# Low parts of the mixer's first 32 weight tiles: made in the first feed-forward block and kept in HBM, or made in the mixer

## The chip, the cores and the metric

The kernel runs on one core of one Trainium2 chip. The metric is the device time of one execution in microseconds (us), as the median of several runs. The engines are TensorE (PE, with its weight load PEld), VectorE (DVE), ScalarE (ACT), GpSimd (POOL) and SyncE (SP), which issues most of the DMAs.

## What is computed

One encoder layer in float32 on 512 tokens of width 1024: a half-step feed-forward block, a mixer of two head groups, a second half-step feed-forward block, and a last norm.

```python
x = x + 0.5 * swiglu(rms_norm(x, ffn1_norm[l]), ffn1_w_gate[l], ffn1_w_up[l], ffn1_w_down[l])
h = rms_norm(x, mix_norm[l])
proj = h @ w_in[l]
qkv_a, z_a, a_a, b_a, qkv_b = jnp.split(proj, split_at, axis=-1)
o_a = gdn_mixer(qkv_a, z_a, a_a, b_a, conv_w[l], a_log[l], dt_bias[l], gdn_norm_w[l])
o_b = dilated_mixer(qkv_b, q_norm_w[l], k_norm_w[l], rel_bias)
x = x + jnp.concatenate([o_a, o_b], axis=-1) @ w_out[l]
...
```

swiglu is (silu(x @ w_gate) * (x @ w_up)) @ w_down with 2816 hidden columns. gdn_mixer is a gated delta rule with four heads of 128, in both directions, with a short convolution, normalized queries and keys, and a triangular solve in each chunk of tokens. dilated_mixer is softmax attention of eight heads of 64 over bands, at three dilations.

## The kernel before

All activations are held transposed, in tiles of 128 features by 512 tokens. Every large product is made of three matmuls (mm3): each factor is split into a high part, rounded to fp32r by a copy on ACT, and a low part, the difference, made by a subtraction on DVE; the three are high by high, high by low and low by high.

In the feed-forward blocks wload (L167) brings a weight tile of 128 x 1024 (raw, two buffers) by a DMA on SP, casts it on ACT (L178) and subtracts on DVE (L179). The first block's gate and up phase, 44 such tiles, lasts until about 250 us, its down phase until 369.6; the mixer lasts until about 734, the second block's gate and up phase until 975.

In the mixer the weights come as 76 tiles of 128 x 512, in the order of the list plan (L185 to L189): two tiles for each projection of ORDER, K0 Q0 K1 Q1 K3 Q2 K2 Z0 Q3 V0 Pa0 V1 Z3 V2 V3 v0 and so on, then 16 for the output projection and 4 for the second block. Tiles 14 and 15 are Z0's, 16 and 17 Q3's, 24 and 25 Z3's, 28 and 29 V3's, 42 and 43 Pa1's. wnext (L211) keeps up to three tiles wsp in use; each is made by split (L228): a cast on ACT (L229), then a subtraction on DVE (L226). The raw data (wrw, two halves of one tile) is loaded ahead by fetch (L198) on SP; a half is free again when its subtraction is done. mm3 uses the high part in its first two matmuls and the low part in the third.

PE's order in the mixer is fixed by hand: interleave runs streams of work by due times, and PEQueue ties each PE instruction to the one before. The other engines' orders are set by a scheduler that weighs when an instruction could run; each engine, and SP's queue, then works strictly in that order. For each head h of the delta rule, decay makes gb on ACT (L561), multiplies it on PE (pdc) and takes the exponential into M; the stage behind the convolution squares keys and queries on ACT (L611), forms pkk and pkq on PE, scales M on DVE (L638), and stores blocks of M into the HBM tensor D1, eight DMAs on SP for each head (L644). When all four heads are there, solve (L824 to L854) loads MM from D1, runs a triangular solve on DVE, stores ZM and ZN and loads M and ZT from them. vtok (L700) are transposed values of the delta rule, made on ACT; the attention's scores go through an exponential into L on ACT (L164).

Of the kernel before, what the change touches and what calls it, by code (L numbers as in the profile page):

```python
# [10 lines left out]
F32 = mybir.dt.float32  # L11
F32R = mybir.dt.float32r
AF = mybir.ActivationFunctionType
ALU = mybir.AluOpType
AX = mybir.AxisListType

P = 128
T = 512
# [15 lines left out]
N_MASK = 768  # L34
LV0, LVG, SCG, ATG = 9.0, 0.625, 0.8, 0.55
GIN, VGO, VGV, PRG, NRG, VTG, VBG, OPG, OTG, FNG, SVG, SSD, SST, VTP, LVH = 9.5, 16.5, 4.0, 0.5, 6.0, 3.5, 3.5, 13.5, 0.75, 10.5, 0.75, 8.0, 0.6, 3.0, 1.3
PRI = 0, 1, 2, 4, 3, 5
ORDER = "rs@1 pa@3 K0 ab gt@2 Q0 K1 bi Q1 pc@3 g0 K3 Q2 K2 g1 Z0 g2 Q3 g3 V0 Pa0 V1 Z3 V2 V3 v0 Pb0 Z2 Z1 Pb1 v1 Pa1 v3 Pa2 Pb2 v2 Pb3 Pa3 oa"

# [50 lines left out]
def encoder_layer(ctx, tc, xT, gu1, dn1, win, wab, wo1, wo2, gu2, dn2, cols, relb, masks, onehot, lnc, sel, out):  # L90
    nc = tc.nc
    te, ve, se, gp, sy = PEQueue(tc, nc.tensor), nc.vector, nc.scalar, nc.gpsimd, nc.sync
# [4 lines left out]
    WF = {"pool": None}  # L97
    tp = ctx.enter_context(tc.tile_pool(name="tp", bufs=2))
    ps = ctx.enter_context(tc.tile_pool(name="ps", bufs=2, space=bass.MemoryType.PSUM))
    dr = ctx.enter_context(tc.tile_pool(name="dr", bufs=1, space=bass.MemoryType.DRAM))  # L100
# [18 lines left out]
    def palt(name):  # L119
        nalt[0] += 1  # L120
        return (pmm, pfl, prg)[nalt[0] % 3](name)

    def tmp(tag, name, n=T, dt=F32, bufs=2):
        return tp.tile([P, n], dt, tag=tag, name=name, bufs=bufs)
# [42 lines left out]
    def wload(src, n, k, low=False, parts=1, then=None):  # L167
        w = n * k
        raw = WF["pool"].tile([P, 1024], F32, tag="raw", name="wraw", bufs=2)
        if low:  # L170
            hi, lo = (wtile(nm) for nm in ("whi", "wlo"))
        else:
            hi, lo = (WF["pool"].tile([P, 1024], F32R, tag=nm, name=nm, bufs=2) for nm in ("whi", "wlo"))
        sv = src.rearrange("p a b -> p (a b)")
        for i in range(parts):
            s = slice(i * w // parts, (i + 1) * w // parts)
            act["lastf"] = sy.dma_start(out=raw[:, s], in_=sv[:, s])
            se.copy(hi[:, s], raw[:, s])  # L178
            ve.tensor_tensor(out=lo[:, s], in0=raw[:, s], in1=hi.bitcast(F32)[:, s], op=ALU.subtract)  # L179
            if then is not None:  # L180
                then(i)
        return (hi[:, :w].rearrange("p (a b) -> p a b", b=k),
                lo[:, :w].rearrange("p (a b) -> p a b", b=k))

    first = {"K": 4, "Q": 0, "V": 8, "Z": 12, "Pa": 16, "Pb": 20, "v": 24}  # L185
    plan = [win[first[u[:-1]] + int(u[-1]), :, 4 * i:4 * i + 4] for u in ORDER.split() if u[:-1] in first
            for i in range(2)]
    plan += [wo1[d, :, 4 * u:4 * u + 4] for d in range(4) for u in range(3)] + [wo2[d] for d in range(4)]
    plan += [gu2[0, j, :, 4 * u:4 * u + 4] for j in range(2) for u in range(2)]  # L189
    nw, got, fetched, ready, wraw = [0], [0, 0], [], [], []  # L190

    def wtile(name, dt=F32R):

        nw[0] += 1
        t, n = ("wb", 1) if nw[0] % 4 == 0 else ("wa", 3)
        return wp.tile([P, 1024], dt, tag=t, name=name, bufs=n)

    def fetch(i):  # L198
        if i < len(plan):
            r = wraw[0][:, i % 2 * T:(i % 2 + 1) * T]  # L200
            sy.dma_start(out=r, in_=plan[i].rearrange("p a b -> p (a b)"))
            fetched.append(r)
# [8 lines left out]
    def wnext():  # L211

        while got[0] < len(plan) and len(ready) < 3:
            t = wp.tile([P, 1024], F32R, tag="wa", name="wsp", bufs=3)
            ready.append(t)
            got[0] += 1
        while got[1] < got[0] - (got[0] < len(plan)):
            i = got[1] - got[0] + len(ready)
            split(ready[i][:, 0:T], ready[i][:, T:2 * T], fetched.pop(0))
            got[1] += 1  # L220
            fetch(got[1] + 1)
        t = ready.pop(0)
        return [t[:, i * T:(i + 1) * T].rearrange("p (a b) -> p a b", b=P) for i in range(2)]

    def sub(o, a, b):
        ve.tensor_tensor(out=o, in0=a, in1=b.bitcast(F32), op=ALU.subtract)  # L226

    def split(hi, lo, src):  # L228
        se.copy(hi, src)  # L229
        sub(lo, src, hi)  # L230

    def mm3(o, wh, wl, rh, rl, start, stop):
        te.matmul(o, lhsT=wh, rhs=rh, start=start, stop=False)
        te.matmul(o, lhsT=wh, rhs=rl, start=False, stop=False)
        act["mm"] = te.matmul(o, lhsT=wl, rhs=rh, start=False, stop=stop)
# [11 lines left out]
    class Norm:  # L247
# [28 lines left out]
        def rstd(self):  # L276
# [4 lines left out]
            preload()  # L281
            rsq(R, pr, 1024.0)

    def ffn(gu, dn, norm, nxt, then=None, late=False, mid=None):
        with tc.tile_pool(name="wf", bufs=2, reuse_waits="tile") as wf, \
                tc.tile_pool(name="hp", bufs=1, reuse_waits="tile") as hp:
            WF["pool"] = wf
            hh = [hp.tile([P, T], F32R, name=f"hh{f}") for f in range(NF)]
            hl = [hp.tile([P, T], F32R, name=f"hl{f}") for f in range(NF)]
            wait = []  # L290
            for f in range(NF):
                pg, pu = palt("pg"), palt("pu")
                for j, pt in ((0, pg), (1, pu)):
                    if f == 0 and late:
                        for u in (0, 4):
                            wh, wl = wnext()
                            for k in range(u, u + 4):
                                mm3(pt, wh[:, k - u], wl[:, k - u], xh[k], xl[k], k == 0, k == NKT - 1)
                        continue
                    first = then if f == 0 and j == 0 else None  # L300
                    wh, wl = wload(gu[f, j], NKT, P, True, 4 if first else 2 if f == 0 else 1, first)
                    for k in range(NKT):
                        mm3(pt, wh[:, k], wl[:, k], xh[k], xl[k], k == 0, k == NKT - 1)
                wait.append((f, pg, pu))
                if f == (0 if late else 1):
                    with tc.issue_after(norm.last.ins):
                        for k in range(NKT):
                            norm.sq(k)
                    norm.rstd()
                if f == 0 and not late:  # L310
                    continue
                for e, pg, pu in wait:
                    g, u = tmp("g", "g"), tmp("u", "u")
                    ve.tensor_tensor(out=g, in0=pg, in1=R, op=ALU.mult)  # L314
                    silu(g, g)
                    ve.tensor_tensor(out=u, in0=pu, in1=R, op=ALU.mult)  # L316
                    ve.tensor_tensor(out=u, in0=u, in1=g, op=ALU.mult)
                    split(hh[e], hl[e], u)
                wait = []
            for d in range(NKT - 1 if late else NKT):  # L320
                pd = palt("pd")
                for f0, n in ((0, 8), (8, 8), (16, 6)):
                    wh, wl = wload(dn[d, :, f0:f0 + n], n, P)
                    for i in range(n):
                        f = f0 + i
                        mm3(pd, wh[:, i], wl[:, i], hh[f], hl[f], f == 0, f == NF - 1)
                ve.scalar_tensor_tensor(out=x[d], in0=pd, scalar=0.5, in1=x[d], op0=ALU.mult, op1=ALU.add)
                nxt(d)
            if late:
                d = NKT - 1  # L330
                ws = [wload(dn[d, :, f0:f0 + n], n, P, f0 == 0) for f0, n in ((0, 8), (8, 8), (16, 6))]
                for i in range(2):
                    pd, s = palt("pd"), slice(256 * i, 256 * i + 256)
                    for f in range(NF):
                        wh, wl = ws[f // 8]
                        mm3(pd[:, 0:256], wh[:, f % 8], wl[:, f % 8], hh[f][:, s], hl[f][:, s], f == 0, f == NF - 1)
                        if (i, f) in ((0, 15), (1, 4)):
                            with tc.issue_after(act["mm"].ins):
                                mid(i)
                    ve.scalar_tensor_tensor(out=x[d][:, s], in0=pd[:, 0:256], scalar=0.5, in1=x[d][:, s], op0=ALU.mult,  # L340
                                            op1=ALU.add)
                nxt(d)
# [15 lines left out]
    def after1(d):  # L358
        n2.add(d)
        sy.dma_start(out=x_d[d], in_=x[d])  # L360

    ffn(gu1, dn1, n1, after1, bring)
    with tc.issue_after(act["lastf"].ins):
        sy.dma_start(out=mk, in_=masks)

    wopen()
    with ExitStack() as mctx:
# [827 lines left out]
        ss = [fins(), chain(), after(), norms(), att(), px()]  # L1195
        interleave([ss[i] for i in PRI])
        te.fixed = False
# [132 lines left out]
```

## Time and profile before

| what | value |
|---|---|
| median of 3 runs | 1108.98 us (1108.09 to 1111.36) |
| the profiled execution | 1109.54 us, its span 1107.8 us |
| mean granted clock of PE | 0.991 |
| PE busy in the span | 1071.4 us, 97% |
| DVE busy | 614.7 us, 55% |
| ACT busy | 443.6 us, 40% |
| HBM read and written | 102.39 and 8.96 MB, 101 GB/s |

The span is what the trace shows of the execution; 1.74 us of its time lie outside. The profile page cuts the span into 40 slices of 27.7 us: PE is at nine tenths or more in all but eight or so, most of which lie in the mixer, where DVE is the next busiest. A timeline row gives an instruction's start, its length, the engine, the line, the operation with its output and inputs, a count where neighbours are put together, and in brackets how long its engine had been idle and what ended that. Clocks are shares of the full 2.4 GHz.

### The profile page before, as it was taken

What the parts mean: (1) busy time and instruction counts of PE and PEld (TensorE: products, weight loads), DVE (VectorE), ACT (ScalarE), POOL (GpSimd) and SP (SyncE); (2) the same over time, 40 slices, a digit from 0 to 9 for tenths busy, and PEclk for the clock granted to TensorE, in tenths of its full rate; (3) what the DMA queues carried; (4) which work ended last, traced back from release to release, by engine and by line L of the source; (5) the groups of instructions that cost most, each with busy time, mean ns of one, the idle gap of its engine ahead of it and who ended that gap; (6) DMA issues with size and microseconds to landing.
All of it is one profiled execution on the core that took longest, in us unless ns stands there. A gap on an engine that the chain in (4) does not pass through costs nothing.

```text
span 1107.8 us, 14127 instructions
## 1 busy us (share of the span) xinstructions
PE 1071.4 (97%) x5394; PEld 881.4 (80%) x5394; DVE 614.7 (55%) x1113; ACT 443.6 (40%) x812; POOL 86.6 (8%) x123
## 2 busy tenths in 40 slices
PE   9999999999999989898999978999999999999996
PEld 7888888888888768776788866878888888888886
DVE  4544444443443497898677888685444444532223
ACT  6432222233222256434675766464232222332221
POOL 3000000000111212610000010000000000001001
PEclk9999999999999999999899999999999999999999
DMA  5222222234433133345422242233222223233332
GB/s 191 97 96 95 95 95 98 97 112 143 121 107 119 35 111 91 105 128 157 72 83 84 70 155 74 69 113 95 95 96 95 97 94 104 94 97 95 96 105 77
DMA packets 53235, 112.27 MB, mean 101 GB/s; under 512 B 17984, under 2 KB 20576, under 8 KB 53168
## 3 DMA queue, kind: packets, MB, share of 16 engines
q1 hardware_dynamic: 48976, 99.50, 29.1%
q0 software_dynamic: 2896, 10.25, 3.1%
q10 hardware_dynamic: 1296, 1.63, 0.5%
q8 instruction: 42, 0.69, 0.3%
q14 instruction: 25, 0.20, 0.1%
HBM read 102.39 MB, written 8.96 MB: 101 GB/s over the span
## 4 chain that ended last, share of the span: by engine, by line
PE 82%; DVE 9%; ACT 3%; issue 3%; DMA 2%; POOL 1%; DVEq 0%; SPq 0%; ACTq 0%; POOLq 0%
PE pg L52 22%; PE pd L52 22%; PE pu L52 22%; PE pc L50 3%; PE pd L50 2%; PE pqk L50 2%; PE ps L50 2%; PE pl L50 1%; DVE wsp L226 1%; PE pout L52 1%; DMA wrw<-in_win 1%; PE pT L50 1%; PE pvb L50 1%; PE pov L50 1%; PE pS L50 1%
## 5 line engine op out<-in xcount | busy, mean ns | idle before, releaser
L178 ACT CAST whi<-wraw 128x1024 fp32r<-128x1024 f32 (+1 forms) x138 | 137.6, 1000 | 424.7 <-issue 174.1
L179 DVE TENSOR_TENSOR wlo<-wraw,whi 128x1024 fp32r<-128x1024 f32 (+1 forms) x138 | 161.1, 1168 | 134.3 <-ACT whi L178 130.1
L52 PE MATMUL pd<-hh,whi 128*128 128x512 f32 (+1 forms) x374 | 141.2, 378 | 0.0
L52 PE MATMUL pd<-hh,wlo 128*128 128x512 f32 (+1 forms) x374 | 140.9, 377 | 0.0
L52 PE MATMUL pd<-hl,whi 128*128 128x512 f32 (+1 forms) x374 | 140.8, 377 | 0.0
L52 PE MATMUL pg<-xh,whi 128*128 128x512 f32 x344 | 135.4, 394 | 0.4 <-ACT whi L178 0.4
L52 PE MATMUL pg<-xl,whi 128*128 128x512 f32 x344 | 135.4, 394 | 0.0
L52 PE MATMUL pg<-xh,wlo 128*128 128x512 f32 x344 | 134.8, 392 | 0.0
L52 PE MATMUL pu<-xh,wlo 128*128 128x512 f32 x344 | 133.9, 389 | 0.0
L52 PE MATMUL pu<-xl,whi 128*128 128x512 f32 x344 | 133.8, 389 | 0.0
L52 PE MATMUL pu<-xh,whi 128*128 128x512 f32 x344 | 133.8, 389 | 0.0
L316 DVE TENSOR_TENSOR u<-pu,R 128x512 f32<-128x512 f32 x44 | 30.4, 691 | 129.6 <-PE pu L52 129.6
L52 PEld LDWEIGHTS pd<-hh,whi 128*128 128x128 f32 x374 | 70.3, 188 | 13.0
L52 PEld LDWEIGHTS pd<-hh,wlo 128*128 128x128 f32 x374 | 70.3, 188 | 13.0
L52 PEld LDWEIGHTS pd<-hl,whi 128*128 128x128 f32 x374 | 70.3, 188 | 12.9
L229 ACT CAST wsp<-wrw 128x512 fp32r<-128x512 f32 x76 | 47.3, 622 | 76.9 <-DMA wrw<-in_win 24.0
L314 DVE TENSOR_TENSOR g<-pg,R 128x512 f32<-128x512 f32 x44 | 30.4, 691 | 84.7 <-PE pg L52 84.7
L52 PEld LDWEIGHTS pg<-xl,whi 128*128 128x128 f32 x344 | 65.1, 189 | 15.3 <-DVE xl L273 1.5
L52 PEld LDWEIGHTS pg<-xh,whi 128*128 128x128 f32 x344 | 65.0, 189 | 14.9 <-ACT whi L178 1.3
L52 PEld LDWEIGHTS pg<-xh,wlo 128*128 128x128 f32 x344 | 64.9, 189 | 13.9 <-DVE wlo L179 0.3
L52 PEld LDWEIGHTS pu<-xh,wlo 128*128 128x128 f32 x344 | 64.6, 188 | 13.7 <-DVE wlo L179 0.2
L52 PEld LDWEIGHTS pu<-xh,whi 128*128 128x128 f32 x344 | 64.6, 188 | 13.4
(296 smaller groups left out, 1697.6 us busy)
## 6 DMA issues: line engine op xcount, KB each, us to landing
wraw<-in_gu SPq DMA_DIRECT2D x84, 512.0 KB, 3.5
wraw<-in_dn SPq DMA_DIRECT2D x32, 512.0 KB, 3.5
wrw<-in_win SPq DMA_DIRECT2D x56, 256.0 KB, 2.7
wraw<-in_dn SPq DMA_DIRECT2D x16, 384.0 KB, 3.2
wrw<-in_wo SPq DMA_DIRECT2D x16, 256.0 KB, 2.7
bw<-vec_d POOLq DMA_DIRECT2D x8, 448.0 KB, 4.3
x<-in_xT SPq DMA_DIRECT2D x8, 256.0 KB, 5.0
x_d<-x SPq DMA_DIRECT2D x8, 256.0 KB, 2.0
```

The source lines that it names most:

```text
L50: self.last = f(*a, **k)
L52: self.last = f(*a, **k)
L178: se.copy(hi[:, s], raw[:, s])
L179: ve.tensor_tensor(out=lo[:, s], in0=raw[:, s], in1=hi.bitcast(F32)[:, s], op=ALU.subtract)
L226: ve.tensor_tensor(out=o, in0=a, in1=b.bitcast(F32), op=ALU.subtract)
L229: se.copy(hi, src)
L314: ve.tensor_tensor(out=g, in0=pg, in1=R, op=ALU.mult)
L316: ve.tensor_tensor(out=u, in0=pu, in1=R, op=ALU.mult)
```

## The change

PUT = 32 tiles get their low part ahead of time. presplit loads a raw tile (praw), casts it into phi on ACT and subtracts in place on DVE; send stores the result in an HBM tensor of its own, ws0 to ws31. share calls presplit between the tiles of the first block's down projection. In the mixer wnext then loads the low half of those tiles from HBM (L241 of the changed kernel) when it takes the buffer, still loads the raw tile and casts it (L247), and subtracts (through sub, L256) for the 44 others alone. The raw buffer of the first 32 is free after the cast.

```diff
--- before.py
+++ after.py
@@ -34,6 +34,7 @@
 N_MASK = 768
 LV0, LVG, SCG, ATG = 9.0, 0.625, 0.8, 0.55
 GIN, VGO, VGV, PRG, NRG, VTG, VBG, OPG, OTG, FNG, SVG, SSD, SST, VTP, LVH = 9.5, 16.5, 4.0, 0.5, 6.0, 3.5, 3.5, 13.5, 0.75, 10.5, 0.75, 8.0, 0.6, 3.0, 1.3
+PUT = 32
 PRI = 0, 1, 2, 4, 3, 5
 ORDER = "rs@1 pa@3 K0 ab gt@2 Q0 K1 bi Q1 pc@3 g0 K3 Q2 K2 g1 Z0 g2 Q3 g3 V0 Pa0 V1 Z3 V2 V3 v0 Pb0 Z2 Z1 Pb1 v1 Pa1 v3 Pa2 Pb2 v2 Pb3 Pa3 oa"
 
@@ -187,6 +188,30 @@
             for i in range(2)]
     plan += [wo1[d, :, 4 * u:4 * u + 4] for d in range(4) for u in range(3)] + [wo2[d] for d in range(4)]
     plan += [gu2[0, j, :, 4 * u:4 * u + 4] for j in range(2) for u in range(2)]
+    ws_d = [dr.tile([P, T], F32, name=f"ws{i}") for i in range(PUT)]
+    made, raws, unsent = [0], [], []
+
+    def send():
+        i, lo = unsent.pop(0)
+        sy.dma_start(out=ws_d[i], in_=lo)
+
+    def presplit():
+
+
+        i = made[0]
+        made[0] += 1
+        if unsent:
+            send()
+        for n in range(0 if i == 0 else i + 2, min(i + 3, PUT)):
+            raws.append(tmp("xp", "praw", T + 4, bufs=3)[:, 0:T] if n % 4 else
+                        WF["pool"].tile([P, T], F32, tag="praw", name="praw", bufs=1))
+            sy.dma_start(out=raws[-1], in_=plan[n].rearrange("p a b -> p (a b)"))
+        lo = raws.pop(0)
+        hi = WF["pool"].tile([P, T], F32R, tag="phi", name="phi", bufs=1)
+        se.copy(hi, lo)
+        ve.tensor_tensor(out=lo.bitcast(F32R), in0=lo, in1=hi.bitcast(F32), op=ALU.subtract)
+        unsent.append((i, lo))
+
     nw, got, fetched, ready, wraw = [0], [0, 0], [], [], []
 
     def wtile(name, dt=F32R):
@@ -212,11 +237,16 @@
 
         while got[0] < len(plan) and len(ready) < 3:
             t = wp.tile([P, 1024], F32R, tag="wa", name="wsp", bufs=3)
+            if got[0] < PUT:
+                sy.dma_start(out=t[:, T:2 * T].bitcast(F32), in_=ws_d[got[0]])
             ready.append(t)
             got[0] += 1
         while got[1] < got[0] - (got[0] < len(plan)):
             i = got[1] - got[0] + len(ready)
-            split(ready[i][:, 0:T], ready[i][:, T:2 * T], fetched.pop(0))
+            raw = fetched.pop(0)
+            se.copy(ready[i][:, 0:T], raw)
+            if got[1] >= PUT:
+                sub(ready[i][:, T:2 * T], raw, ready[i][:, 0:T])
             got[1] += 1
             fetch(got[1] + 1)
         t = ready.pop(0)
@@ -280,6 +310,10 @@
                 te.matmul(pr, lhsT=ones, rhs=self.tail, start=False, stop=True)
             preload()
             rsq(R, pr, 1024.0)
+
+    def share(step):
+        while made[0] < PUT and made[0] * 23 < PUT * step:
+            presplit()
 
     def ffn(gu, dn, norm, nxt, then=None, late=False, mid=None):
         with tc.tile_pool(name="wf", bufs=2, reuse_waits="tile") as wf, \
@@ -321,6 +355,8 @@
                 pd = palt("pd")
                 for f0, n in ((0, 8), (8, 8), (16, 6)):
                     wh, wl = wload(dn[d, :, f0:f0 + n], n, P)
+                    if not late:
+                        share(3 * d + f0 // 8 + 1)
                     for i in range(n):
                         f = f0 + i
                         mm3(pd, wh[:, i], wl[:, i], hh[f], hl[f], f == 0, f == NF - 1)
@@ -360,6 +396,8 @@
         sy.dma_start(out=x_d[d], in_=x[d])
 
     ffn(gu1, dn1, n1, after1, bring)
+    while unsent:
+        send()
     with tc.issue_after(act["lastf"].ins):
         sy.dma_start(out=mk, in_=masks)
```

PE's order is the same before and after. On the other engines the scheduler sets a new one. SP, first block, gate and up phase, a piece of the changed kernel (praw is a raw tile of the mixer's, ws the HBM tensors, numbered from 102 for tile 0); before, one row of 42 wraw loads stands there:

```order
L178 DMA wraw<-in_gu 128x1024
L208 DMA praw<-in_win 128x512
L196 DMA ws_107<-praw 128x512
L208 DMA praw<-in_win 128x512
L196 DMA ws_108<-praw 128x512
L178 DMA wraw<-in_gu 128x1024
L208 DMA praw<-in_win 128x512
L196 DMA ws_109<-praw 128x512
```

All 32 presplits stand in this phase, not in the down projection: the scheduler moved them ahead.

SP in the mixer, around the four blocks of eight stores of M into D, first before and then after (ws_118 is the low half of tile 16, ws_127 that of tile 25):

```order
L201 DMA wrw<-in_win 128x512 x12
L644 DMA D_2564<-M 32x4x32 x8
L201 DMA wrw<-in_win 128x512 x6
L644 DMA D_2564<-M 32x4x32 x8
L201 DMA wrw<-in_win 128x512
L644 DMA D_2564<-M 32x4x32 x8
L201 DMA wrw<-in_win 128x512 x2
L644 DMA D_2564<-M 32x4x32 x8
L201 DMA wrw<-in_win 128x512 x2
L824 DMA MM<-D_2564 64x1024 x2
```

```order
L682 DMA D_2788<-M 32x4x32 x8
L241 DMA wsp<-ws_118 128x512
L241 DMA wsp<-ws_119 128x512
L226 DMA wrw<-in_win 128x512 x2
...
L682 DMA D_2788<-M 32x4x32 x8
L241 DMA wsp<-ws_127 128x512
L241 DMA wsp<-ws_128 128x512
L862 DMA MM<-D_2788 64x1024 x2
L226 DMA wrw<-in_win 128x512
```

The loads of the low halves now stand directly behind the blocks, ahead of the raw loads.

ACT in the mixer, at the first groups of gb (the decay of head 0) and, further on, at the first two exponentials of the attention (L<-L,mx), before and after:

```order
L561 ACTIVATE gb<-mk,gh 128x128
L164 ACTIVATE cs<-pcs 128x96
L153 ACT_TABLE_LOAD
L153 ACTIVATE kT<-kT 128x512
L153 ACTIVATE qT<-qT 128x512
L164 ACT_TABLE_LOAD
L164 ACTIVATE M<-pdc 128x512
L430 ACTIVATE kT<-xp,col 128x512
L561 ACTIVATE gb<-mk,gh 128x128 x3
```

```order
L599 ACTIVATE gb<-mk,gh 128x128 x4
L247 CAST wsp<-wrw 128x512
L468 ACTIVATE qT<-xp,col 128x512
L247 CAST wsp<-wrw 128x512
L165 ACTIVATE cs<-pcs 128x96
L154 ACT_TABLE_LOAD
```

```order
L229 CAST wsp<-wrw 128x512
L809 CAST KA_4100<-kn 64x512
L809 CAST KA_4101<-kn 64x512
L868 ACTIVATE tts<-pl 128x256 x2
L164 ACTIVATE L,den<-L,mx 128x512
L476 CAST vb<-ptv 128x4x64 x2
L164 ACTIVATE L,den<-L,mx 128x512
```

```order
L847 CAST KA_4324<-kn 64x512
L847 CAST KA_4325<-kn 64x512
L906 ACTIVATE tts<-pl 128x256 x2
L165 ACTIVATE L,den<-L,mx 128x512
L514 CAST vb<-ptv 128x4x64 x2
L165 ACTIVATE L,den<-L,mx 128x512
L247 CAST wsp<-wrw 128x512 x3
```

All four gb now stand ahead of the two table loads, and the casts of tiles 43 to 45 behind the second exponential, where that of tile 43 stood ahead of both.

## Rows read from the trace of the kernel before

**Rows 1.** Stretches: bounds, length, busy us (instructions) by engine, clock, DMA share, GB/s.

```profile
369.60:734.00 364.40, 339.32 (x2129) 276.05 (x2129) 291.00 (x728) 205.42 (x505) 52.06 (x86) 0.98 0.34 97
...
20.00:117.00 97.00, 97.00 (x425) 79.57 (x425) 46.94 (x57) 34.06 (x43) 3.41 (x3) 1.00 0.30 98
```

**Rows 2.** Timeline of PE in the mixer: start, length, operation, idle before and its releaser.

```profile
411.93 0.73 PE L50 MATMUL pdc<-gb,excr 128*128 128x512 f32 x2 [2.88 <-ACT gb L561]
...
429.72 0.39 PE L50 MATMUL pz<-xh,wsp 128*128 128x512 f32 x1
...
435.16 0.39 PE L50 MATMUL pc<-xh,wsp 128*128 128x512 f32 x1
...
452.72 1.16 PE L50 MATMUL pkq<-qT,kT 128*128 128x128 f32 x8 [3.54 <-DVE M L638]
...
453.63 0.63 PE L50 MATMUL pc<-xh,wsp 128*128 128x512 f32 x1
...
457.05 0.70 PE L50 MATMUL pc<-xh,wsp 128*128 128x512 f32 x2
...
472.50 0.47 PE L50 MATMUL pz<-xh,wsp 128*128 128x512 f32 x1 [0.67 <-DVE t L788]
...
488.63 0.74 PE L50 MATMUL pc<-xh,wsp 128*128 128x512 f32 x2 [1.18 <-DVE wsp L226]
...
527.19 1.11 PE L50 MATMUL ptv<-mk,vbT 128*128 128x128 f32 x4 [3.55 <-ACT vtok L700]
...
543.56 0.39 PE L50 MATMUL pqk<-xh,wsp 128*128 128x512 f32 x1
```

**Rows 3.** The same view as rows 1, ten microseconds each, two places in the mixer.

```profile
449.00:459.00 10.00, 6.46 (x27) 5.17 (x26) 8.93 (x24) 2.90 (x13) 6.82 (x9) 0.83 0.34 92
...
519.00:529.00 10.00, 5.92 (x25) 4.04 (x24) 5.01 (x8) 6.73 (x15) 0.00 (x0) 0.82 1.01 214
```

**Rows 4.** Operations on the mixer's tiles: count, ns min/median/max, first and last start.

```profile
L229 ACT CAST wsp<-wrw x76: 602/621/677, 253.3 to 737.1; 128x512 fp32r<-128x512 f32 x76
L226 DVE TENSOR_TENSOR wsp<-wrw,wsp x76: 637/684/1528, 253.9 to 738.2; 128x512 fp32r<-128x512 f32 x76
```

**Rows 5.** Timeline of ACT in the mixer, columns as in rows 2.

```profile
406.04 1.28 ACT L153 ACT_TABLE_LOAD   x1
...
410.90 0.97 ACT L561 ACTIVATE gb<-mk,gh 128x128 fp32r<-128x128 f32 x3
...
437.15 0.62 ACT L229 CAST wsp<-wrw 128x512 fp32r<-128x512 f32 x1 [1.59 <-DMA wrw<-in_win]
...
443.81 0.62 ACT L229 CAST wsp<-wrw 128x512 fp32r<-128x512 f32 x1 [1.16 <-PE pkq L50]
...
477.31 0.62 ACT L229 CAST wsp<-wrw 128x512 fp32r<-128x512 f32 x1 [2.09 <-DMA wrw<-in_win]
...
521.78 0.62 ACT L229 CAST wsp<-wrw 128x512 fp32r<-128x512 f32 x1 [3.73 <-DMA wrw<-in_win]
...
545.16 0.72 ACT L164 ACTIVATE L<-L,mx 128x512 f32<-128x512 f32 x1 [0.63 <-DVE mx L1084]
```

**Rows 6.** Timeline of SP's DMA issues in the mixer, columns as in rows 2.

```profile
429.03 4.70 SPq L644 DMA_DIRECT2D D<-M  x8
...
470.64 3.71 SPq L644 DMA_DIRECT2D D<-M  x8
...
515.74 0.54 SPq L201 DMA_DIRECT2D wrw<-in_win  x1
```

**Rows 7.** Timeline of ACT in the first gate and up phase.

```profile
48.41 1.05 ACT L178 CAST whi<-wraw 128x1024 fp32r<-128x1024 f32 x1 [3.12 <-PE pg L52]
...
53.85 1.05 ACT L178 CAST whi<-wraw 128x1024 fp32r<-128x1024 f32 x1 [3.86 <-issue]
```

**Rows 8.** Page, part 5: group, busy us, mean ns, idle time before, releaser.

```profile
L179 DVE TENSOR_TENSOR wlo<-wraw,whi 128x1024 fp32r<-128x1024 f32 (+1 forms) x138 | 161.1, 1168 | 134.3 <-ACT whi L178 130.1
```

**Rows 9.** Page, part 6: DMA issues, KB each, us to landing.

```profile
wraw<-in_gu SPq DMA_DIRECT2D x84, 512.0 KB, 3.5
```

## The prediction

> **What bounds the kernel now.** I read the stretches first. From 20 to 117 us PE is busy 97.00 of 97.00 us; over the mixer (369.6 to 734) it is busy 339.32 of 364.40 us, so all that an edit can win lies in 25.1 us of idle time there, and in the matmuls that run slowly behind the longer idles [rows 1]. Second, PE's timeline in the mixer. Three idles are long: 2.88 us (ended by ACT's gb), 3.54 us (DVE's M) and 3.55 us (ACT's vtok); one, 1.18 us, is ended by the subtraction of a weight tile itself [rows 2]. Third, the clock there: the ten microseconds around each of the two 3.5 us idles show a granted clock of 0.83 and 0.82, a mix of the full level, 2.4 GHz, and the half, 1.2 GHz [rows 3]. The price of that: from 453.63 to 457.05 us eight matmuls start, 0.43 us each; from 429.72 to 435.16 there are 24, 0.227 us each [rows 2]. Eight times 0.2 us is 1.6 us per such idle. A tile is twelve matmuls, 2.72 us.
>
> The engines ahead of PE in the mixer are DVE, busy 291.00 us, and ACT, 205.42 [rows 1]. DVE spends 0.684 us on each tile's subtraction and ACT 0.621 on its cast, 76 of each [rows 4].
>
> **The change, part by part.** *The work made early.* Thirty-two subtractions leave the mixer: 32 x 0.684 = 21.9 us of DVE [rows 4]. The same 32 casts (19.9 us of ACT) and subtractions (21.9 us of DVE) are added before it, with 32 loads and 32 stores of 256 KB on SP's queue. The source writes them in the down projection; in the order of instructions they stand in the gate and up phase, some two per weight tile from the fourth tile to about the nineteenth. There DVE is busy 46.94 and ACT 34.06 of 97 us [rows 1], so both have room. What the added work must fit into is the lead of a weight tile. One is cast every 5.44 us (48.41 to 53.85) [rows 7]; cast and subtraction take 1.05 + 1.17 [rows 7, 8], which leaves 3.2 us ahead of PE, against two small casts and two small subtractions per tile, 1.3 + 1.4 us, on two engines. A tile's load is issued when the subtraction two tiles earlier frees its buffer, some 8.7 us before its own cast (5.44 x 2 less 1.05 and 1.17), and lands in 3.5 [rows 9]. The queues have 0.30 of the DMA engines busy at 98 GB/s [rows 1]; 16.8 MB more in about 97 us is 173 GB/s, which by the same ratio makes 0.83. I cost this at nothing: PE's own 5.4 us a tile is the cover. Without it, see rival C.
>
> *The pages against it.* The raw load at 515.74 us landed only by 521.78, 6.0 us, where the DMA share stood at 1.01 [rows 3, 5, 6]; a 512 KB load at a share of 0.30 takes 3.5 [rows 1, 9]. The Trainium skill (DMA: Bandwidth & Descriptors, Latency and other measured facts) says that reaching HBM costs about 0.2 us on average and 2 us under high load. By that, a gate and up load would land 1.8 us later, in an estimated 5.3 us; the 8.7 us still hold it, and the sum stays, but C loses part of its margin.
>
> *A new load on SP.* In the mixer each of the 32 tiles gets a load of its low half, which waits until PE is done with the buffer three tiles earlier, so two tiles, 5.4 us, ahead of its use. On SP it stands in order with the raw loads, and with the blocks of eight D stores of the four heads. Behind the first block (429.03, 4.70 us long) stand the low halves of tiles 16 and 17; behind the last (470.64, 3.71 us) those of 25 and 26 [rows 6]. What comes out of such a place shows in the casts now: behind the first block the raw load reaches ACT at 437.15 us, after 1.59 us of waiting, 3.4 after the block's end at 433.73; behind the last at 477.31, 3.0 after 474.35 [rows 5, 6]. Today two tiles of lead cover that; the low half has no such lead. Tile 16 starts at 435.16, so its low half would be 437.1 - 435.2 = 1.9 us late; I take +1.3, since the block waits for M on DVE and DVE loses subtractions ahead of it (bounds 0 and 1.9, or more if PE comes earlier: rival B). Tile 25 starts 2.72 us after 472.50 [rows 2], at 475.2; its low half would come at 477.3, 2.1 late; I take +1.6 (bounds 0.5 and 2.5).
>
> *The 2.88 us idle.* gb stands on ACT behind two table loads of 1.28 us (one stands in the rows) and waits at 410.90 [rows 5]. After the change four gb stand ahead of them, because the chain of g has fewer subtractions ahead of it on DVE. What PE meets next is the following group of four, 4 x 0.32 = 1.3 us: the idle falls by 1.6, and with it the slow matmuls, 1.5 by the price above. -3.1 (bounds -4.4, all of it, and 0).
>
> *The 3.54 us idle.* PE waits for head 1's M, at the end of a chain that starts on ACT behind the casts of tiles 19 and 20 (the latter at 443.81, after waiting 1.16) [rows 5], and runs over DVE, 8.93 of 10 us busy there [rows 3]. Raw buffers are now free after the cast, not after a subtraction; one subtraction leaves the chain itself and several leave the queue ahead. I take 2 to 2.4 us off the idle and so the slow matmuls too: -2.2 - 2.1 = -4.3 (bounds -5.6 and 0). Part comes back one head later, where the M chain is then late: +0.5.
>
> *The 1.18 us idle* ends with a subtraction that is gone: -1.2 (bounds -1.2 and 0). Four of the subtractions inside the triangular solve go as well, 4 x 0.68 = 2.7 us of its chain.
>
> *The 3.55 us idle.* vtok waits behind a cast that waits 3.73 us for the slow load of 515.74 [rows 5, 6]; that load is behind the solve's stores, which now come earlier. But the order puts another table load ahead of these casts, and the solve's result must be stored and read back before PE can go on. I take -2.6, and -1.9 for the clock, +1.0 given back at the read back: -3.5 (bounds -5 and +2).
>
> *Tiles 43 to 45.* Their casts move on ACT behind the second exponential of L, which starts at 545.16 and lasts 0.72 us with its row sum behind it [rows 5]. PE reaches tile 43 at 543.56 [rows 2], right behind the scores which that exponential needs. The cast then ends at 545.16 + 0.82 + 0.62 = 546.6, and the tile's subtraction is still in the mixer: 3.0 us, partly overlapped with the first matmuls. +2.8 (bounds 0 and 4.6, with the clock).
>
> The sum: -3.1 + 1.3 - 4.3 + 0.5 + 1.6 - 1.2 - 3.5 + 2.8 = -5.9 us. The profiled execution took 1109.54 us and becomes 1103.6; the median of the runs, 1108.98, lies 0.56 lower: **1103 us**. A measurement of this kernel can tell a difference of about 0.3%, 3.3 us, from none: same is 1105.7 to 1112.3.
>
> **The rivals.** *A, nothing net.* The idles at 411.93 and 452.72 shrink, but PE only arrives earlier at tiles 16 and 25, whose low halves come when SP's blocks let them, and at the next head's M. Then -3.1, -4.3, +0.5, +1.3 and +1.6 make 0 and not -4.0, and what is left is -1.2 - 3.5 + 2.8 = -1.9: 1107 us. For it: blocks and loads share one queue. Against it: the block's own start follows M, which DVE now reaches sooner. *B, slower.* The last block ends at 474.35 as now. Tile 25 then starts at 477.3 whatever PE gained before it, 2.1 us later than now, and after an idle as long as PE's gain plus 2.1 the clock falls (1.6); the vtok chain keeps its idle, tile 43 costs 2.8, the 1.18 us idle goes: 2.1 + 1.6 + 2.8 - 1.2 = +5.3, or 1114 us. It decides from the point where that block ends less than about 1 us sooner than now. *C, the early work isn't hidden.* SP issues in order, and each store of a low part waits for its subtraction, with weight loads queued behind. Three presplits are in flight; with a landing of 3.4, cast and subtraction of 1.3 and about 1 us of queueing, two need 3.8 us of a 5.44 us tile. At a landing of 6.0 [rows 5, 6] two need 5.5, and at 7 us 6.2, 0.1 to 0.75 us more than the tile has, over sixteen tiles 1.5 to 12 us; with 6 taken from the sum above 1109 us. *D, more.* All three long idles become so short that the clock stays up, and SP's blocks come early enough for tiles 16 and 25: -5.9 - 1.3 - 1.6 = -8.8, and -1.5 more from the idles themselves: 1099 us.
>
> **How the numbers follow.** The forecast (1100 to 1105.6) has 0.42, D 0.13, A 0.23, B 0.15, C 0.07. Faster: 0.42 + 0.13 = 0.55. Within 0.3%: A and C, 0.30. Slower: B, 0.15. The range leaves out the far half of B and of D: from D's 1099 less 1.5 for the bounds of the 3.54 us idle, 1097.5, to 1113, just under B's 1114, with all of A and C inside.
>
> **What would show it.** Right, if PE's idles that gb, M and vtok end are each under 2.5 us and the granted clock stays at 1.00 around them; if PE shows idles of 1 to 2 us ended by a DMA of a low half at tiles 16 and 25, and one of about 2.8 us ended by ACT's cast at tile 43; if gate and up stays at 97.00 busy of 97 us from 20 to 117. Wrong in the size: idles of over 3 us at tiles 16 or 25 with a clock under 0.9 (B), the same total idle time in the mixer as now (A), or gate and up ending later than now (C). The sum as a whole is wrong if DVE still ends PE's waits between 370 and 490 us with its 20 subtractions or more gone.

## The result, and the profile after

The changed kernel takes 1127.03 us (median of 4 runs, 1125.58 to 1128.9), the kernel before, timed beside it, 1110.17. The ratio is 1.016, with a 95% interval of 1.0138 to 1.0181: 17 us slower, where 6 us faster was forecast and a range up to 1113 us was given.

The page of the changed kernel begins with its span, 18.5 us longer, and PE's busy time, 9.9 us more for the same matmuls:

```profile
span 1126.3 us, 14355 instructions
...
PE 1081.3 (96%) x5394; PEld 888.8 (79%) x5394; DVE 615.9 (55%) x1113; ACT 460.5 (41%) x844; POOL 88.9 (8%) x123
```

The stretches, columns as in rows 1 and 3, say where. The first two lines are the first gate and up phase, the third the mixer, the others ten microseconds each:

```profile
20.00:117.00 97.00, 89.06 (x368) 70.50 (x367) 61.39 (x82) 47.98 (x71) 5.24 (x9) 0.95 0.76 246
117.00:249.80 132.80, 132.80 (x587) 109.98 (x586) 61.69 (x73) 39.48 (x49) 0.00 (x0) 1.00 0.29 96
369.60:734.00 364.40, 339.29 (x2106) 277.02 (x2105) 262.77 (x680) 198.67 (x496) 53.74 (x87) 0.96 0.39 114
530.00:540.00 10.00, 4.94 (x19) 3.98 (x17) 5.36 (x10) 7.09 (x18) 0.00 (x0) 0.67 0.93 118
550.00:560.00 10.00, 7.19 (x110) 5.47 (x107) 3.26 (x9) 4.04 (x11) 0.00 (x0) 0.70 0.19 55
560.00:570.00 10.00, 10.00 (x120) 7.99 (x119) 5.11 (x11) 3.69 (x9) 0.00 (x0) 0.62 0.19 54
```

From 20 to 117 us PE was busy all 97.00 us before [rows 1]; now it idles 7.9 us there, and the granted clock is 0.95. The rest of gate and up is undisturbed. The first matmul of the down phase starts at 262.8 us and not 249.7: 13.1 us are lost before the mixer begins.

PE's timeline, with the idle time and what ended it in brackets, in gate and up (two of six such waits) and in the mixer (the long ones):

```profile
46.52 0.79 PE L53 MATMUL pg<-xh,whi 128*128 128x512 f32 x1 [3.39 <-ACT whi L179]
...
49.51 0.80 PE L53 MATMUL pg<-xh,wlo 128*128 128x512 f32 x1 [1.77 <-DVE wlo L180]
...
426.53 0.73 PE L51 MATMUL pdc<-gb,excr 128*128 128x512 f32 x2 [1.00 <-ACT gb L599]
...
446.73 0.73 PE L51 MATMUL pc<-xh,wsp 128*128 128x512 f32 x2 [1.62 <-DMA wsp<-ws]
...
461.44 1.77 PE L51 MATMUL pkq<-qT,kT 128*128 128x128 f32 x8 [2.23 <-DVE M L676]
...
484.99 0.73 PE L51 MATMUL pz<-xh,wsp 128*128 128x512 f32 x2 [0.51 <-DMA wsp<-ws]
...
535.73 1.11 PE L51 MATMUL ptv<-mk,vbT 128*128 128x128 f32 x4 [5.06 <-ACT vtok L738]
...
554.83 0.79 PE L51 MATMUL pqk<-xh,wsp 128*128 128x512 f32 x1 [2.81 <-ACT wsp L247]
```

In gate and up PE waits for ACT's cast whi and DVE's difference wlo of the weight tiles. In the mixer, the idle at gb is now 1.00 us (before 2.88), the one at DVE's M 2.23 (3.54), the 1.18 us one is gone, and two new ones are ended by the DMA of a low half: 1.62 us at tile 16, 0.51 at tile 25. The idle at vtok is 5.06 us (before 3.55). At tile 43 there is a new one of 2.81 us, ended by ACT's cast; the two stretches around and behind it show a clock of 0.70 and 0.62 (in steps of two microseconds: 0.50 from 554 to 566, 1.00 again from 568). Before, PE started that tile at 543.56 without an idle [rows 2].

The same instruction's start in both traces gives the running difference: +13.1 us at the mixer's first tile, +8.7 at head 1's pkq (452.72 before, 461.44 now), +7.0 where the idle at vtok begins, +8.5 where it ends, and +16.6 some 50 us on (570.51 and 587.14). So up to the solve's result the mixer wins 6 us, then loses 1.5 us at vtok and 8 us around tile 43. The last 2 us come at an idle that both kernels have, ended by DVE's xa: 2.37 us at 683.76 before, 2.29 us at 700.95 now. The first matmul behind it takes 0.50 us before and 0.79 now, and the difference goes from +17.2 to +18.7 us.

### The profile page after: what moved, and what is told of

It is laid out like the page before. It is cut to its first block, busy times and chain, and to the rows that moved or that the text cites. A ratio compares the mean times of both kernels' runs of the same rounds, so it can differ in the third digit from the quotient of the medians.

```text
span 1126.3 us, 14355 instructions
## 1 busy us (share of the span) xinstructions
PE 1081.3 (96%) x5394; PEld 888.8 (79%) x5394; DVE 615.9 (55%) x1113; ACT 460.5 (41%) x844; POOL 88.9 (8%) x123
## 4 chain that ended last, share of the span: by engine, by line
PE 75%; DVE 9%; DMA 7%; ACT 4%; issue 2%; POOL 1%; SPq 0%; DVEq 0%; ACTq 0%; POOLq 0%
PE pd L53 21%; PE pu L53 17%; PE pg L53 17%; PE pc L51 4%; PE pqk L51 3%; PE pd L51 3%; DMA praw<-in_win 3%; DMA ws<-praw 2%; PE ps L51 2%; PE pl L51 1%; PE pvb L51 1%; PE pT L51 1%; PE pS L51 1%; PE pov L51 1%; DMA x<-in_xT 1%
## 5 line engine op out<-in xcount | busy, mean ns | idle before, releaser
L53 PEld LDWEIGHTS pd<-hh,whi 128*128 128x128 f32 x374 | 70.3, 188 | 13.1
L53 PEld LDWEIGHTS pg<-xh,wlo 128*128 128x128 f32 x344 | 65.7, 191 | 17.8 <-DVE wlo L180 3.7
L247 ACT CAST wsp<-wrw 128x512 fp32r<-128x512 f32 x76 | 47.0, 619 | 73.7 <-DMA wrw<-in_win 28.2
L53 PEld LDWEIGHTS pu<-xh,wlo 128*128 128x128 f32 x344 | 64.5, 188 | 14.6 <-DVE wlo L180 1.4
L53 PEld LDWEIGHTS pu<-xl,whi 128*128 128x128 f32 x344 | 64.6, 188 | 13.3
```

The lines of the kernel that those rows point to most:

```text
L53: self.last = f(*a, **k)
L247: se.copy(ready[i][:, 0:T], raw)
```

## The experiments

In the table the ratios are those to the kernel before, run beside each.

| kernel | median, us | ratio, 95% interval |
|---|---|---|
| changed | 1127.03 | 1.016 (1.0138 to 1.0181) |
| e1, presplits alone | 1124.59 | 1.0132 (1.0114 to 1.0149) |
| e2, their DMAs alone | 1110.06 | 1.0011 (0.9993 to 1.0028) |
| e3, the mixer alone | 1113.57 | 1.0035 (1.0019 to 1.0051) |
| e4, presplits in down | 1112.11 | 1.0023 (1.0004 to 1.0042) |
| e5, changed, cast 43 early | 1120.31 | 1.0093 (1.0059 to 1.0126) |
| e6, e4 with cast 43 early | 1108.70 | 1.0001 (0.9977 to 1.0024) |
| e7, e6 with cast 42 late | 1104.20 | 0.9944 (0.9922 to 0.9965) |
| e8, e1 with casts on POOL | 1123.21 | 1.0123 (1.0092 to 1.0155) |
| e9, early work without DMA | 1110.14 | 1.0000 (0.9981 to 1.0019) |
| e10, before, cast 42 late | 1110.05 | 1.0004 (0.9990 to 1.0019) |
| e11, e7 again | 1103.55 | 0.9946 (0.9926 to 0.9965) |

**e1: the presplits alone.** The mixer takes no low half from HBM.

```diff
-            if got[0] < PUT:
-                sy.dma_start(out=t[:, T:2 * T].bitcast(F32), in_=ws_d[got[0]])
...
-            if got[1] >= PUT:
+            if True:
                 sub(ready[i][:, T:2 * T], raw, ready[i][:, 0:T])
```

> The 32 presplits and their stores stay in the first gate and up phase, in the changed kernel's order there; the mixer loads no low half and makes all 76 by subtraction on DVE, as before. Theory 1 (13 us of the loss are the early work, whatever the mixer does): gate and up ends 12 to 14 us later than in the kernel before, the mixer is unchanged, 1121 to 1124 us. Rival (most of the loss is in the mixer, and the early part costs what stands visibly idle there, 8 us or less): 1113 to 1118 us.

1124.59 us, 14.6 us more than before by the ratio, a little above what theory 1 gave and far from its rival. The stretch from 20 to 117 us looks as in the changed kernel:

```profile
20.00:117.00 97.00, 90.25 (x372) 71.78 (x372) 63.19 (x82) 47.73 (x69) 5.12 (x9) 0.95 0.77 247
```

The early work costs its 13 to 15 us whatever the mixer does.

**e3: the mixer alone.** One presplit is made, and all 32 loads read its result.

```diff
-        while made[0] < PUT and made[0] * 23 < PUT * step:
+        while made[0] < 1:
...
-                sy.dma_start(out=t[:, T:2 * T].bitcast(F32), in_=ws_d[got[0]])
+                sy.dma_start(out=t[:, T:2 * T].bitcast(F32), in_=ws_d[0])
```

> Only one presplit is made; the mixer of the changed kernel is kept, with its 32 loads of low halves, all of them from that one stored tile (so the low parts of the other 31 are wrong, the work is the same). Theory 2 (the mixer loses by itself: 6 us won up to the solve, then lost again at vtok and, with the slow clock behind it, at tile 43): 1112 to 1116 us. Rival (with gate and up undisturbed the mixer is worth what was forecast): 1102 to 1105 us.

1113.57 us, 3.9 us more than before. e1 and e3 add up to 18.5 us, near the 17.8 of the changed kernel by its ratio. The PE rows at vtok and at tile 43, and the ten microseconds behind the second:

```profile
521.64 0.66 PE L51 MATMUL ptv<-mk,vbT 128*128 128x128 f32 x4 [3.73 <-ACT vtok L738]
...
538.60 0.80 PE L51 MATMUL pqk<-xh,wsp 128*128 128x512 f32 x1 [2.80 <-ACT wsp L247]
```

```profile
540.00:550.00 10.00, 10.00 (x118) 7.46 (x116) 4.88 (x10) 3.80 (x8) 0.00 (x0) 0.65 0.32 107
```

The idle of 2.80 us at tile 43 is there without any early work, and so is the low clock behind it. The mixer by itself was not worth the forecast.

**e2: the transfers alone.** As e1, without the early casts and subtractions. SP's order is that of the changed kernel up to about 40 us; from there the scheduler set another one, with the same loads and stores.

```diff
-        hi = WF["pool"].tile([P, T], F32R, tag="phi", name="phi", bufs=1)
-        se.copy(hi, lo)
-        ve.tensor_tensor(out=lo.bitcast(F32R), in0=lo, in1=hi.bitcast(F32), op=ALU.subtract)
```

> As the run with presplits alone, with the 32 early casts and subtractions left out: only the 32 loads and 32 stores stand in SP's order (the stored data is then the raw tile, which nobody reads). Theory 1a (ACT's order: weight casts stand behind small casts that wait for their raw load): without the casts gate and up ends within 2 us of the kernel before, 1109 to 1112 us. Rival 1b (the transfers themselves, at a DMA share near 0.8, and SP's order bring the weight tiles late): gate and up still ends 8 to 13 us later, 1117 to 1124 us.

1110.06 us, no measurable loss, at a DMA share of 0.78:

```profile
20.00:117.00 97.00, 95.80 (x419) 78.60 (x420) 47.88 (x58) 33.75 (x43) 3.92 (x9) 1.00 0.78 259
```

PE idles 1.2 us there, once. 16.8 MB more on the queues do not by themselves make the weight tiles late. What e2 doesn't test is SP's order: its stores no longer wait for a subtraction, and behind about 40 us the order is another.

**e8: the early casts on POOL.** This asks whether ACT's order alone does it.

```diff
-        se.copy(hi, lo)
+        gp.tensor_copy(hi, lo)
```

> As the run with presplits alone (mixer as before), with the 32 early casts made on POOL instead of ACT; the 32 subtractions stay on DVE. Theory 1a (weight casts held up behind small casts on ACT): gate and up ends at most 4 us late, 1110 to 1114 us. Rival 1c (it is DVE's order: the small subtractions, waiting, stand ahead of the weight tiles' subtractions): gate and up still 8 us or more late, 1118 us or above.

1123.21 us: rival 1c, no better than e1. PE's two longest idles (3.42 and 2.33 us, the longer shown) are now ended by DVE's wlo, and some 11 us ahead of the first of them a small subtraction on DVE waits 2.46 us for its cast, which has waited 3.67 us for its raw load:

```profile
47.50 0.79 PE L53 MATMUL pg<-xh,wlo 128*128 128x512 f32 x1 [3.42 <-DVE wlo L180]
```

```profile
35.69 0.62 POOL L211 CAST phi<-praw 128x512 fp32r<-128x512 f32 x1 [3.67 <-DMA praw<-in_win]
...
36.34 0.69 DVE L212 TENSOR_TENSOR praw<-praw,phi 128x512 fp32r<-128x512 f32 x1 [2.46 <-POOL phi L211]
```

Behind that subtraction stand, on DVE, the steps that ACT's first gates wait for (5.31 us, at 40.53), and behind those the next weight tile's work. So ACT was not the only engine on which weight work queued up; freeing it moved the waits to DVE.

**e9: the early work without its DMAs.** The same 32 casts and 32 subtractions, two to a weight tile, on data that lies in SBUF (x[7]); nothing is loaded, stored or used.

```diff
+        with tc.issue_after(act["whis"][7 + i // 2].ins):
+            se.copy(hi, x[7])
+        ve.tensor_tensor(out=lo.bitcast(F32R), in0=x[7], in1=hi.bitcast(F32), op=ALU.subtract)
```

> The kernel before, with 32 small casts on ACT and 32 small subtractions on DVE added in the first gate and up phase, two to a weight tile as in the changed kernel, but on data that is already there and without any load or store; the results go nowhere. Theory 1d (what delays the weight tiles is that early work waits for its raw loads while weight work queues behind it): no wait, so gate and up ends at most 3 us late, 1108 to 1113 us. Rival 1e (the 42 us of added work itself is too much for ACT and DVE there): gate and up 8 us or more late, 1117 us or above.

1110.14 us, a ratio of 1.0000:

```profile
20.00:117.00 97.00, 97.00 (x426) 79.63 (x425) 67.30 (x89) 51.95 (x75) 3.69 (x9) 1.00 0.29 99
```

PE is busy 97.00 of 97.00 us, with DVE at 67.30 and ACT at 51.95, more than in the changed kernel (61.39 and 47.98). The work fits, as the prediction had it. Alone, the transfers (e2) and the work each cost nothing that can be measured; together, with work that waits for its transfers, they cost 14.6 us (e1).

**e4: the presplits in the down phase.** Each raw load is tied behind the weight load ahead of it in the source.

```diff
+            with tc.issue_after(act["lastf"].ins):
-            sy.dma_start(out=raws[-1], in_=plan[n].rearrange("p a b -> p (a b)"))
+                sy.dma_start(out=raws[-1], in_=plan[n].rearrange("p a b -> p (a b)"))
```

> The changed kernel with each raw load of a presplit tied behind the weight load that stands before it in the source, so that all presplits lie in the down phase. If the place is the cause: gate and up ends at 249.8 as before, the down phase hides the work (its tile takes 5.4 us as well, but no gates and exponentials share ACT and DVE), and the mixer's loss stays: 1112 to 1116 us. If the work can't be hidden beside either phase: the down phase gets longer by 5 us or more, 1118 us or above.

1112.11 us. The down phase:

```profile
249.80:369.60 119.80, 118.86 (x523) 97.76 (x522) 60.47 (x68) 49.41 (x71) 11.07 (x15) 1.00 0.75 247
```

PE idles 0.9 us of 119.80. Yet the early casts wait for their raw loads in this phase too, by the groups of what ended ACT's idle time before phi, us and times:

```profile
  DMA praw<-in_win: 31.7, 22
```

That is more than in gate and up (23.1 us, 14 times, below). One of them is longer than those shown from gate and up, with a weight tile's cast behind it, and PE doesn't stop there:

```profile
292.30 0.62 ACT L212 CAST phi<-praw 128x512 fp32r<-128x512 f32 x1 [5.00 <-DMA praw<-in_win]
292.83 1.05 ACT L179 CAST whi<-wraw 128x1024 fp32r<-128x1024 f32 x1
```

The same waits cost about a microsecond here. The engines carry less in this phase (DVE is busy 60.47 of 119.80 us, against 61.39 of 97), but that this is the reason is argued and was not tried apart. What is left of the 1112 us fits the mixer's loss in e3.

**e5 and e6: the cast of tile 43.** It is put back ahead of the first exponential on ACT, in the changed kernel (e5) and in e4 (e6); the copies into vb are tied behind it in the same way.

```diff
+            if got[1] == 43:
+                act["c43"] = act["cast"]
...
-                lx(L, L, AF.Exp, bias=mx[:, 32 + n:33 + n], accum_out=den[:, n:n + 1])
+                with behind():
+                    lx(L, L, AF.Exp, bias=mx[:, 32 + n:33 + n], accum_out=den[:, n:n + 1])
```

> The changed kernel with one thing moved back: on ACT the cast of tile 43 stands ahead of the first exponential of the attention instead of behind the second. Theory 3 (the 2.81 us idle at tile 43 costs itself and about 4.7 us of matmuls at the half clock behind it, since PE then works on small matmuls too): 7 us less than the changed kernel, 1118 to 1121 us. Rival (the idle alone counts, the slow stretch comes anyway from the idle at vtok): 1123 to 1125 us.

> The same move, with the presplits in the down phase. If the two causes add up (gate and up 13 us, tile 43 about 7 us): 1104 to 1107 us. If the time comes back at the next wait: 1109 to 1112 us.

e5 takes 1120.31 us, 6.7 less than the changed kernel, as theory 3 has it; its five runs, 1117.57 to 1126.38 us, reach over the rival's range, and in the profiled one, the fastest, the idle at vtok is shorter too (3.57 us). e6 takes 1108.70, between its two expectations; that is 3.4 less than e4, but the intervals of the two ratios overlap. In e6 PE's rows at vtok and at tile 43, and their stretches:

```profile
524.45 1.11 PE L51 MATMUL ptv<-mk,vbT 128*128 128x128 f32 x4 [5.44 <-ACT vtok L745]
...
542.43 0.73 PE L51 MATMUL pqk<-xh,wsp 128*128 128x512 f32 x2 [1.13 <-DVE wsp L262]
```

```profile
520.00:530.00 10.00, 5.55 (x17) 4.55 (x18) 6.42 (x11) 8.32 (x20) 0.00 (x0) 0.66 1.02 134
...
540.00:550.00 10.00, 8.44 (x125) 6.52 (x124) 7.54 (x17) 5.43 (x12) 0.00 (x0) 1.00 0.26 81
```

The idle at tile 43 is down to 1.13 us, ended by that tile's subtraction, and the clock there is full, 1.00. The idle at vtok and the low clock there (0.66) are as in e4 (5.60 us and 0.66). So the slow stretch behind tile 43 doesn't come from vtok: it is gone when the idle at tile 43 is short. That a short idle always leaves the clock up is not shown; e11 below has a slow stretch of another kind.

**e7 and e11: the cast of tile 42.** In e6, it is put behind the vtok group on ACT.

```diff
-                se.mul(vtok[:, h, c, :], pt[:, c * P:(c + 1) * P], ivn[:, h * 4 + c:h * 4 + c + 1])
+                act["vtok"] = se.mul(vtok[:, h, c, :], pt[:, c * P:(c + 1) * P], ivn[:, h * 4 + c:h * 4 + c + 1])
...
+            with tc.issue_after(act["vtok"].ins) if got[1] == 42 else ExitStack():
```

> As the run before, and on ACT the cast of tile 42 stands behind the vtok group, not ahead of it. Theory 4 (vtok is late because that cast waits for its raw load, which is slow beside the solve's stores): the idle at vtok goes from 5.6 to 3 us or less, 2 to 5 us less in all, 1100 to 1104 us. Rival (vtok waits for other things that come as late, or the solve's result is late anyway): within 1 us of the run before.

> The presplits in the down phase, the casts of tiles 43 and 42 moved, once more, beside the kernel before with its cast 42 moved. If the low halves from HBM are worth something by themselves: 2 to 5 us under that kernel, 1101 to 1105 us. If the order of ACT was all there was to win: the two within 1.5 us of each other.

1104.20 and 1103.55 us: 4.5 to 5 us less than e6, and 6 us less than the kernel before (ratio 0.9944 and 0.9946). PE's rows:

```profile
520.84 0.66 PE L51 MATMUL ptv<-mk,vbT 128*128 128x128 f32 x4 [1.93 <-ACT vtok L746]
...
538.19 0.73 PE L51 MATMUL pqk<-xh,wsp 128*128 128x512 f32 x2 [1.14 <-DVE wsp L263]
```

The idle at vtok is 1.93 us, not 5.44 (1.10 in e11). vtok was late because of a cast whose tile PE reaches only 12 us later (532.12 and 544.40 in the changed kernel).

**e10: the same move in the kernel before.**

> The kernel before with one change: on ACT the cast of tile 42 stands behind the vtok group. If theory 4 holds for the kernel before too: its 3.55 us idle at vtok falls by 1.5 to 3 us, with less slow clock behind it, 1104 to 1108 us. If the order only matters with the low halves in HBM: 1109 to 1111 us.

1110.05 us, a ratio of 1.0004, outside what theory 4 gave: the idle at vtok only falls to 2.90 us, and nothing is won. The second row is ACT's, ahead of the vtok group:

```profile
525.70 0.66 PE L50 MATMUL ptv<-mk,vbT 128*128 128x128 f32 x4 [2.90 <-ACT vtok L701]
...
520.80 0.63 ACT L153 ACTIVATE vT<-vT 128x512 f32<-128x512 f32 x1 [3.29 <-DVE vT L435]
```

Without the cast, ACT waits there 3.29 us for DVE to finish vT; in e7 it waits 0.63 us for the same. That fits a DVE which in the kernel before still makes all the low halves, but was not tried apart.

So that order alone doesn't make e7: with the casts of tiles 43 and 42 in their places and the presplits in the down phase, the low halves from HBM are worth about 6 us (e11 against e10, 1103.55 and 1110.05).

## Why the prediction was wrong

**The step that failed first: "I cost this at nothing".** The early work was set against the lead of a weight tile, 3.2 us, and against busy shares, as if it were ready when its turn came. It isn't: it waits for loads of its own, and ACT and DVE work in order. What stood idle before phi and its subtraction in the changed kernel, and until what (us, times):

```profile
  ACT phi L211: 26.7, 21
  DMA praw<-in_win: 23.1, 14
  DVE praw L212: 8.5, 9
```

ACT waits 23.1 us, in 14 places, for a raw tile, and DVE 26.7 us, in 21 places, for the cast behind it; another 8.5 us are waits for phi's one buffer. Each such wait holds up the weight work queued behind it. On DVE, and on ACT up to the tile at which PE idles longest:

```profile
34.75 0.69 DVE L212 TENSOR_TENSOR praw<-praw,phi 128x512 fp32r<-128x512 f32 x1 [3.52 <-ACT phi L211]
...
35.70 1.23 DVE L180 TENSOR_TENSOR wlo<-wraw,whi 128x1024 fp32r<-128x1024 f32 x1 [0.26 <-ACT whi L179]
```

```profile
34.09 0.62 ACT L211 CAST phi<-praw 128x512 fp32r<-128x512 f32 x1 [3.59 <-DMA praw<-in_win]
34.62 1.04 ACT L179 CAST whi<-wraw 128x1024 fp32r<-128x1024 f32 x1
...
42.45 0.62 ACT L211 CAST phi<-praw 128x512 fp32r<-128x512 f32 x1 [3.51 <-DVE g L348]
43.09 1.28 ACT L154 ACT_TABLE_LOAD   x1
44.38 1.15 ACT L154 ACTIVATE g<-g 128x512 f32<-128x512 f32 x2
45.44 1.03 ACT L179 CAST whi<-wraw 128x1024 fp32r<-128x1024 f32 x1
```

Between the two, SP's issues, and the raw load's piece in the chain of work that ended last (start, us):

```profile
36.95 0.33 SPq L178 DMA_DIRECT2D wraw<-in_gu  x1
37.33 0.42 SPq L208 DMA_DIRECT2D praw<-in_win  x1
```

```profile
37.33 5.05 DMA praw<-in_win
```

At 34.09 us the small cast has waited 3.59 us for its load, and the weight tile's cast whi follows at 34.62, its wlo at 35.70. The end of that wlo, 36.93, frees a weight buffer; only then does SP send the next weight load and, behind it, the raw load of 37.33, which lands 5.05 us later. The phi of 42.45 stands for it (the row names DVE's g, which ended at the same time; the chain goes through the load), and behind that phi come a table load, the first two gates and the next whi, at 45.44. PE was done with the tile before at 43.13 and idles 3.39 us, then 1.77 for the wlo. A wait of 3.5 us is more than the whole lead of 3.2 us. Behind these idles the granted clock is 0.50 from 46 to 52 us. All this comes to 13.1 us, of which 7.9 are idle. e2 and e9 show that neither the transfers nor the work do this apart; e1 that both do it without the mixer; e8 that it is not ACT alone.

Rival C had the right place, at 0.07 and 1.5 to 12 us. It let SP's order throttle the weight loads. No whi in this stretch waits for its own load, though these loads now take longer (20 to 117 us; the median was 3.4 before):

```profile
DMA to landing us min/median/max: 3.4/4.7/5.6
```

But SP's order has a part in it, the other way round: the raw load stands behind a weight load that waits for its buffer. No run changed that order by itself, so its share of the 13 us stays open.

The prediction took 3.4 us for a raw tile's landing; it was 4.5 by the profile's page. The Trainium skill (DMA: Bandwidth & Descriptors, Latency and other measured facts) has the latency to HBM grow from 0.2 to 2 us under load; 4.5 against the 2.7 us of the same transfer in the mixer before agrees with it, and so do the weight loads, 4.7 against 3.4. That ACT and DVE take their queue strictly in order stands in the Trainium skill as well (TensorE: Matmul & The Clock Gate, in its architectural detail), and these rows agree: no whi starts ahead of a phi that stands before it.

**Tile 43: the idle right, its price wrong.** Forecast +2.8 us, measured an idle of 2.81 us. But the clock was counted only in a bound (up to 4.6). With the clock at 0.50 from 554 to 566 us, the place cost 8.1 us from the end of the vtok idle to 587 us; moving the cast wins 6.7 us in e5 and 3.4 in e6, the second not clear of the noise.

**vtok: the sign was wrong.** Forecast -3.5, measured +1.5 at its end. ACT's rows at vtok and at tile 43:

```profile
532.12 0.62 ACT L247 CAST wsp<-wrw 128x512 fp32r<-128x512 f32 x1 [2.62 <-DMA wrw<-in_win]
...
534.55 1.64 ACT L738 ACTIVATE vtok<-ptr,ivn 128x128 f32<-128x128 f32 x6
...
553.45 0.72 ACT L165 ACTIVATE L<-L,mx 128x512 f32<-128x512 f32 x1 [0.63 <-DVE mx L1122]
...
554.17 1.12 ACT L247 CAST wsp<-wrw 128x512 fp32r<-128x512 f32 x2
```

The cast at 532.12 waits for a raw load, as the one at 521.78 did before [rows 5], and not one vtok stands ahead of it: two steps of rsb and one of nw (2 us) come first, then vtok at 534.55. The prediction saw the order change and still took the gain of an earlier solve. The solve's stores did come earlier, but PE came earlier too, and what ends the idle is that load, landing beside the stores (DMA share 0.93). The idle is not the same in every run of this order (3.73 us in e3, 3.57 in e5, 5.60 in e4, 5.44 in e6), so the size of the loss is partly chance; the forecast gain is in none of them. e7 shows the cause: with the cast moved, the idle is 1.93 us. That is shown for this mixer; in the kernel before the same move wins nothing (e10).

**What held.** The idle at gb: forecast 1.3 us, measured 1.00. Tile 16: forecast +1.3, measured 1.62, ended by the low half's DMA. The 1.18 us idle at a subtraction: gone. The idle at M fell by 1.3 us where 2 to 2.4 were forecast, and the clock still fell there. Tile 25 cost 0.51 us, a third of what was forecast. Up to the vtok idle the sum of the mixer's terms was -3.1 + 1.3 - 4.3 + 0.5 + 1.6 - 1.2 = -5.2 us; the trace has -6.1. That the two are so near is partly luck. The slow matmuls behind M, 2.1 us of the sum, did not go: behind pkq the difference falls only from 8.7 to 8.5 us (472.50 before, 481.03 now). Tile 25 cost 1.1 us less than forecast, and 0.75 us were won between 491 us and the vtok idle, for which the sum had no term. Rival B's blocked queue at tile 25 did not happen.

## What to carry to other kernels

Work moved to where an engine has room still needs its data to be there: in an in-order queue, a filler that waits for its own DMA takes its wait from the lead of everything behind it, so set the filler's waits, and not only its busy time, against that lead. A long wait is not yet a loss (e4), but it has to be looked at. Look in the changed order for every cast or copy that waits for a load, and ask who stands behind it and when its result is needed; two such casts moved here, with the presplits in the down phase, turned a loss into a gain. An idle of PE is priced with the clock behind it, and that price changes from one execution to the next.

## What the runs showed of the hardware

The granted clock took longer to come back after the idle at tile 43 than after that at M before. Before the change, behind the idle of 3.54 us at M, PE's matmuls were back at their full pace at 457.05, 4.3 us after the idle's end at 452.72 [rows 2]; behind the 2.81 us idle at tile 43 the clock was 0.50 from 554 to 566 us, where PE's time goes in part to 32 x 32 matmuls, though PE counts as busy all of 556 to 566. Why it stays low there was not tried.

The length of an idle doesn't settle whether the clock falls. In e10 it stayed at 1.00 behind the 2.90 us at vtok, in the kernel before behind the 2.37 us at xa, where the changed kernel's 2.29 us brought the half pace. In e11 it fell with next to no idle: behind the 1.10 us at vtok PE ran at full pace, came to 32 x 32 matmuls at 522.56, idled 0.32 us at 524.38 and then not at all until 538; the clock was 0.50 from 526 to 538:

```profile
517.87 0.65 PE L51 MATMUL ptv<-mk,vbT 128*128 128x128 f32 x4 [1.10 <-ACT vtok L746]
...
524.38 0.69 PE L51 MATMUL pl<-ZT,M 32*32 32x32 f32 x16 [0.32 <-DMA ZT<-ZN]
```

```profile
530.00:540.00 10.00, 9.25 (x77) 6.92 (x76) 2.66 (x8) 3.24 (x8) 0.00 (x0) 0.55 0.00 0
```

In e7, the same kernel, no such stretch follows (1.00 from 530 to 540). Runs of one kernel differ by some 7 us (1100.29 to 1107.07 in e11), and such stretches can be a part of that. Nor was it tried whether raw tiles loaded further ahead would let the early work stay in gate and up.
